# Second feed-forward product: loads pinned in program order, late operand tiles split inside the first unit, side work traced further behind its loads

## The chip, the core and the metric

The kernel runs on one core of one Trainium2 chip. TensorE (PE in the profile) multiplies matrices, with its weight loads shown apart (PEld); VectorE (DVE), ScalarE (ACT) and GpSimd (POOL) do elementwise work; SyncE (SP) issues nearly all DMAs here, one after the other. The metric is the device time of one execution in microseconds, from runs without a profiler; a further execution is profiled.

## The reference

One layer of a decoder trunk: a feed-forward block, a token mixer with two branches, a second feed-forward block, and a final norm, for 1024 prompt tokens and 64 sample tokens (8 sequences of 8). What matters here is the feed-forward block, which occurs twice:

```python
D_MODEL, D_FF = 1024, 2816

def swiglu(x, w_in, w_out):
    gu = x @ w_in
    g, u = gu[..., :D_FF], gu[..., D_FF:]
    return (jax.nn.silu(g) * u) @ w_out

x = x + 0.5 * swiglu(rmsnorm(x, norm_ffn1[l]), ffn1_w_in[l], ffn1_w_out[l])
...
x = x + mix
x = x + 0.5 * swiglu(rmsnorm(x, norm_ffn2[l]), ffn2_w_in[l], ffn2_w_out[l])
```

All values are float32. `x @ w_in` is the first product of the block, `(...) @ w_out` the second.

## The kernel before

**Number format.** A float32 operand is split into a rounded part and a remainder, both in the format that TensorE multiplies at full rate, and a product is the sum of three matmuls: rounded by rounded, remainder of x by rounded weight, rounded x by remainder of the weight. The rounded part is made by an activation on ScalarE, the remainder by a subtraction on VectorE. For weights of the second product these are `wh` and `wl` in `parts` (L782, L783); for its operand tiles they are `hh` (or `hp`) and `hr` in `split_X` (L764, L765). The activation of `split_X` is pinned, that is, queued behind everything traced before it on ScalarE.

**Tiling.** Tokens lie along the free dimension, in two halves of 512 and 576 columns; channels lie along the 128 partitions. Both products of a block are computed by a two-by-two scheme with seven products of half-size blocks instead of eight, so combinations of weights and of operands stand in place of the blocks themselves. In the second product the operand combinations have been written to DRAM (`hblock`) by the first product: eleven tiles of 128 x 544 for each of the products "1" to "7" (`NK2 = 11`, `N2 = 544`).

**The second product** (`second`) runs the products in the order 1, 2, 5, 6, 4, 7, 3. Each has four units (`m` = 0 to 3); a unit multiplies the eleven operand tiles by three chunks of weights (four, four and three tiles, `kb` = 0, 4, 8) for both halves, 66 matmuls, into two PSUM banks, and `leave` adds the result to the tiles `xt`. Product 3 is the exception: it runs its four units for one half and then for the other.

**Its weights** (`weights`, `raw`) are loaded from DRAM chunk by chunk (L771), when the unit is traced. Products 1, 2 and 4 use a block as it is. Product 5 adds two blocks on GpSimd (L800) into a tile that is held until the end; product 6 subtracts another block from the held tile (L804); `fourth` (L816), after each unit of product 4, turns the held tile into what product 3 uses; product 7 subtracts two blocks (L809). There are six buffers for raw weights and three each for `wh` and `wl`, a unit's worth.

**Its operand tiles** are loaded by `fetch_X` (L757). While unit m of a product runs, up to three tiles of the next product are fetched, at most `AHEAD[p]` in all; the rest follow at the start of that product. Its first eight tiles are split at the start of the product, the others in its first unit, before the third chunk (`kb == 8`). For product 3 all are fetched and split before its first unit.

**Old x.** The residual lies in DRAM (`xspill`). In product 6, `old` loads a quarter of it before each unit (L822), and `leave` loads another quarter into `b[:, s_]` once the unit's `add(a[:, s_], b[:, s_])` (L855) has read what stood there (L874). Product 7 loads two quarters a unit.

**The order of the work.** A scheduler reorders the instructions of each engine at compile time, by their readiness in its own model and by program order; on the chip each engine then keeps that order. This holds for SP's queue of DMAs too: an instruction there that waits for a semaphore holds up those behind it. `pin(...)` takes an instruction out of this freedom: it is queued behind the instruction traced last on the same engine. Before the change, `pin` stands at the activation of `split_X`, at the side splits and at the sums of hidden tiles and their puts.

**Side work.** A modelled clock of TensorE (`pe[0]`) advances with every matmul traced; generators wait for it (`yield 4.0` means 4 modelled us) and are stepped by `tick`. Two of them run during the first product of the first block: `turn_x` loads blocks of x (L992), waits, transposes them on TensorE (L170) and writes them to `xspill`; `part` (L312 to L321) loads weights that are used later, waits `PART_W`, splits them, writes both parts to DRAM and waits `PART_PACE`. Its 28 chunks there are followed by `finish(side)` ahead of the second product, which steps what is left without waiting.

**The last hidden pair.** The hidden tiles of the last pair of the first product (`hlast`) are put to DRAM, summed on GpSimd and put again (`hidden_odd`, `pair_sums`, L729, L708), all traced ahead of the first unit of product 1.

Of the kernel before, what the change touches and what calls it, by code (L numbers as in the profile page):

```python
# [14 lines left out]
P = 128  # L15
# [28 lines left out]
N_FP = 4  # L44
NK2, N2, HALF_AT = NFF // 2, 544, (0, 256)
H_AT, H_PACE, H_OUT, H_AGAIN, H_LOAD = 4.0, 0.5, 3.0, 100.0, 5.0
AHEAD = {'2': 11, '5': 11, '6': 8, '4': 8, '7': 10, '3': 10}
STEP = (5.0, 3.8)
STEP_S = 1.0
POST, RIPE = 1.0, 3.0  # L50
# [7 lines left out]
TURN_AT, CONST_AT = 60.0, 40.0  # L58
HP, HP_ST, HP_EV = 40, 0, 60
SETS = (((0,), (1,), (2,), (3,)), ((0, 1), (2,), (3,)))  # L60
PART_AT, PART_W, PART_PACE = 20.0, 4.0, 3.0


@with_exitstack
def tile_hybrid_pool_ssd_macaron(
# [11 lines left out]
    dma = nc.sync.dma_start  # L77
# [7 lines left out]
    def nm(s):  # L85
        uid[0] += 1
        return f"{s}_{uid[0]}"

    def act(shape=(P, 576), dt=F32, name="a"):
        return sp.tile(list(shape), dt, tag="act", bufs=N_ACT, name=nm(name))  # L90

    def pair(n, name="hl"):
        t = sp.tile([P, 2, 576], F32R, tag="pair", bufs=N_PAIR, name=nm(name))
        return t[:, 0, :n], t[:, 1, :n], t
# [16 lines left out]
    def fx(dt=F32, name="x"):  # L111
        if stage["name"] == "mix":
            return act((P, 576), dt, name)
        return stage["p"].tile([P, 592], dt, tag="fx", bufs=N_FX, name=nm(name))

    def psum(tag="ps", name="ps"):
        npd = stage["npd"]
        return stage["ps"].tile([P, 512], F32, tag=tag, bufs=npd if tag == "pd" else 8 - npd, name=nm(name))
# [35 lines left out]
    def finish(c):  # L154
        while not c.done:
            c.step()
# [8 lines left out]
    def mm(out, lhsT, rhs, start=True, stop=True, free=False):  # L165
        T.matmul(out, lhsT, rhs, start=start, stop=stop, skip_group_check=free)  # L166
        pe[0] += max(out.free_size(), 64) / 2400.0 * (1 if rhs.dtype == F32R else 4)

    def tr(out, in_, idn):
        T.transpose(out, in_, idn)  # L170
        pe[0] += 0.107
# [81 lines left out]
    xspill = [[dp.tile([P, NTOK[h]], F32, tag=f"xs{h}_{m}", name=f"xspill{h}_{m}") for m in range(KD)] for h in HALVES]  # L253
# [52 lines left out]
    pin = tc.keep_in_program_order  # L306
# [374 lines left out]
    hblock = {}  # L681
    for i in range(NK2):
        for ps_ in ("1" if i else "18", "23", "75", "46"):
            t = dp.tile([P, len(ps_), N2], F32, tag=f"hb{ps_}_{i}", name=f"hb{ps_}_{i}")
# [3 lines left out]
    even, hsums = [None, None], []  # L688
# [46 lines left out]
    hlast = []  # L735

    def second(wo, after, half):

        wv = wo.rearrange("(i two p) c -> two p i c", two=2, p=P)
# [7 lines left out]
        def fetch_X(p, n):  # L747
            for k in range(len(X[p]), min(len(X[p]) + n, NK2)):
                if k >= 4:
                    a, r = act((P, 576), F32R, "hh"), act((P, 576), name="hr")  # L750
                elif p == "1":
                    a, r = fx(F32R, "hh"), fx(name="hr")
                else:
                    a, r, _ = pair(576, "hp")
                    r = r.bitcast(F32)
                a, r = a[:, :N2], r[:, :N2]
                dma(r, hblock[p, k])  # L757
                raws.append((k, r, a))
                X[p].append((a, r.bitcast(F32R)))

        def split_X(below=NK2):
            while raws and raws[0][0] < below:
                _, r, a = raws.pop(0)
                pin(S.activation(a, r, AF.Copy))  # L764
                V.tensor_tensor(r.bitcast(F32R), r, a.bitcast(F32), op=ALU.subtract)  # L765

        def raw(par, mh, m, kb, nk, t=None):
            if t is None:
                t = sp.tile([P, 4 * P], F32, tag="wraw", bufs=N_RAW, name=nm("wraw"))[:, : nk * P]
            c0 = (mh * 4 + m) * P  # L770
            dma(t.rearrange("p (k c) -> p k c", c=P), wv[par][:, kb : kb + nk, c0 : c0 + P])  # L771
            return t

        def ring(tag, nk):
# [43 lines left out]
        def old(m, q, col):  # L818
            t = act((P, 576), name="xo")
            for h in HALVES:  # L820
                n, at = NPAIR[h], HALF_AT[h]
                dma(t[:, at : at + n], xspill[h][4 * q + m][:, col * n : (col + 1) * n])  # L822

            def put():
                for h in HALVES:
                    n, at = NPAIR[h], HALF_AT[h]
                    o = xt[h][4 * q + m][:, col * n : (col + 1) * n]
                    G.tensor_tensor(o, o, t[:, at : at + n], op=ALU.add)

            late_.append(put)  # L830

        def unit(p, m, hs, ws):
            pts = [psum("pd", "po" + p)[:, : NPAIR[h]] for h in hs]
            for kb, nk, wh, wl in ws:
                if kb and len(hs) == 2 and (p, m) == ("1", 0):
                    split_X(kb + 4)
                elif kb == 8 and len(hs) == 2:
                    split_X()
                for kk in range(nk):
                    k = kb + kk  # L840
                    for j, (W_, lo_) in enumerate(((wh, 0), (wh, 1), (wl, 0))):
                        for h, pt in zip(hs, pts):
                            at = HALF_AT[h]
                            mm(pt, W_[:, kk, :], X[p][k][lo_][:, at : at + NPAIR[h]],
                               start=k == 0 and j == 0, stop=k == NK2 - 1 and j == 2)
                    tick()
            for h, pt in zip(hs, pts):
                leave(p, m, h, pt)

        def leave(p, m, h, pt):  # L850
            n, at = NPAIR[h], HALF_AT[h]
            f, s_ = slice(0, n), slice(n, 2 * n)

            def add(out, prior):
                V.scalar_tensor_tensor(out, pt, 0.5, prior, op0=ALU.mult, op1=ALU.add)  # L855

            if p == "1":
                if T1[m] is None:
                    T1[m] = act((P, 576), name="t1")
                S.activation(T1[m][:, at : at + n], pt, AF.Copy, scale=0.5)  # L860
                return
            if p == "2":
                xt[h][m] = fx(name="x")
            elif p == "5":
                xt[h][4 + m] = fx(name="x")
            t, a, b = T1[m][:, at : at + n], xt[h][m], xt[h][4 + m]
            if p == "2":
                add(a[:, f], t)
            elif p == "5":
                add(b[:, s_], t)  # L870
            elif p == "6":
                add(a[:, s_], b[:, s_])
                add(b[:, f], t)
                dma(b[:, s_], xspill[h][4 + m][:, s_])  # L874
            elif p == "4":
                add(b[:, f], b[:, f])
                G.tensor_tensor(b[:, s_], b[:, s_], a[:, s_], op=ALU.add)
            elif p == "7":
                add(b[:, f], b[:, f])
                add(b[:, s_], b[:, s_])  # L880
            else:
                add(a[:, s_], a[:, s_])

        fetch_X("1", NK2)
        split_X(4)
        while hlast:
            hlast.pop(0)()
        while hsums:
            finish(hsums.pop(0))
        for p, nxt in zip(order[:-1], order[1:]):  # L890
            if p != "1":
                split_X(8)
            fetch_X(p, NK2)
            for m in range(4):
                if p == "6":
                    old(m, 0, 0)
                elif p == "7":
                    old(m, 1, 0)
                    old(m, 0, 1)
                unit(p, m, HALVES, weights(p, m))  # L900
                if p == "4":
                    fourth(m)
                while late_:
                    late_.pop(0)()
                n = AHEAD[nxt] - len(X[nxt])
                fetch_X(nxt, min(n, 3))
        fetch_X("3", NK2)
        split_X()
        for h in HALVES:
            half(h, xt[h])  # L910
        kept = {m: [] for m in range(4)}
# [74 lines left out]
    def turn_x(h):  # L986

        for q in range(2):
            x = [fx(name="xr") for _ in range(4)]
            for src, c0, c in blocks_of(h):  # L990
                t = fx(name="xin2")
                dma(t[:c, :512], src[:, q * 512 : (q + 1) * 512])  # L992
                yield 4.0
                pt = psum("ps", "ptr")
                for k in range(4):
                    tr(pt[:, k * P : k * P + c], t[:c, k * P : (k + 1) * P], ident[:c, :c])
                for k in range(4):
                    (V.tensor_copy if k % 2 else S.copy)(x[k][:, c0 : c0 + c], pt[:, k * P : k * P + c])
                yield 2.0
            for k in range(4):  # L1000
                dma(xspill[h][q * 4 + k], x[k][:, : NTOK[h]])
# [859 lines left out]
    for h in HALVES:  # L1861
# [4 lines left out]
        if h == 1:  # L1866
            o = []
            prep2.append((start(norm_parts(reload(0), 0, i_g2, o, 2.0)), o))
            c = prep2[0][0]
# [125 lines left out]
```

## Time and profile before

| | us |
|---|---|
| Median of 3 runs | 2934.36 |
| Lowest and highest run | 2931.92 and 2937.41 |
| The profiled execution | 2929.76 |
| Its span, first to last instruction | 2927.9 |
| Second product of the first block, first matmul | 541.1 |
| Second product of the second block, last matmul | 2911.9 |

Mean granted clock of TensorE over the span: 0.985 of full speed. DMA: 515.26 MB at a mean of 176 GB/s.

How to read it: the span is a little shorter than the time of the same execution, since the start and end of the program lie outside it. An engine's busy time says how much work it has; what a change is worth is read from the idle time of the engine that sets the end, stretch by stretch, and from who ended that idle time. In rows of the timeline the bracket at the end gives the idle time of the engine ahead of the instruction and what ended it. A name such as `PE po L166` is engine, tile written and line; L166 is the one line that issues every matmul, so the tile (`po` for the second product, `pw` for the first) tells where it belongs.

### The profile page before, as it was taken

To read this page: it belongs to the slowest core of one execution; us is meant where nothing else is said; L and a number is where in the kernel's file an instruction comes from. 1 tells how busy PE (TensorE), PEld (TensorE's weight loads), DVE (VectorE), ACT (ScalarE), POOL (GpSimd) and SP (SyncE) were. 2 spreads that over 40 slices of the span, in tenths; PEclk is the share of its full clock that TensorE was granted. 3 is DMA by queue.
4 is the path that set the end of the run, shared out by engine and by line. 5 is a ranking of instruction groups with operands and counts; after the bars stand their busy time and mean duration, and the time that the engine had idled before them with its cause. 6 is when DMAs were issued, how large, how long until landed. Compare 5 with 4: busy or idle time off the path is not lost. (4 is left out here: it accounts for less than half of the span.)

```text
span 2927.9 us, 54569 instructions
## 1 busy us (share of the span) xinstructions
PE 2787.8 (95%) x19834; PEld 2608.0 (89%) x19834; DVE 1851.4 (63%) x2848; ACT 1400.3 (48%) x3086; POOL 1367.9 (47%) x1424
## 2 busy tenths in 40 slices
PE   7999999989999999999989999898999999999998
PEld 6988999889879999999988887677999999999897
DVE  6665655667684486867666767866665444456665
ACT  5444444533454555554546566576234444444343
POOL 5456666255342364554632333323124675661651
PEclk9999999999999999999999999999999999999999
DMA  4576543778445555543366567786674332336873
GB/s 132 162 228 219 187 132 99 214 221 243 149 114 162 162 162 185 172 150 127 98 227 212 186 215 243 243 257 193 227 248 145 116 124 90 101 119 201 246 227 102
DMA packets 567438, 515.26 MB, mean 176 GB/s; under 512 B 37876, under 2 KB 436072, under 8 KB 567160
## 3 DMA queue, kind: packets, MB, share of 16 engines
q1 hardware_dynamic: 567152, 511.77, 55.8%
q8 instruction: 156, 2.56, 0.4%
q14 instruction: 114, 0.93, 0.1%
q10 hardware_dynamic: 16, 0.00, 0.0%
HBM read 363.51 MB, written 148.36 MB: 175 GB/s over the span
## 5 line engine op out<-in xcount | busy, mean ns | idle before, releaser
L166 PE MATMUL pw<-X,wh 128*128 128x288 f32 (+2 forms) x2832 | 628.3, 310 | 6.1 <-ACT v L568 3.5
L166 PEld LDWEIGHTS pw<-X,wh 128*128 128x128 f32 x2832 | 463.0, 190 | 28.7 <-ACT v L568 4.5
L166 PE MATMUL pw<-X,wl 128*128 128x288 f32 (+1 forms) x1644 | 473.6, 288 | 0.0
L452 DVE TENSOR_TENSOR wl<-s,wh 128x512 fp32r<-128x512 f32 x288 | 233.1, 810 | 258.8 <-ACT wh L451 241.7
L166 PE MATMUL pw<-hl,wh 128*128 128x256 f32 (+1 forms) x1536 | 393.0, 328 | 3.9 <-DVE t L572 3.5
L445 POOL TENSOR_TENSOR s<-wraw,wraw 128x512 f32<-128x512 f32 x144 | 201.2, 1397 | 340.5 <-DVE wl L452 218.2
L166 PE MATMUL pw<-hi,wh 128*128 128x288 f32 x1120 | 331.4, 296 | 2.6 <-DVE t L606 2.6
L166 PE MATMUL pw<-hi,wl 128*128 128x288 f32 x1120 | 330.3, 295 | 0.0
L166 PE MATMUL pw<-lo,wh 128*128 128x288 f32 x1120 | 330.0, 295 | 0.0
L166 PEld LDWEIGHTS pw<-X,wl 128*128 128x128 f32 x1644 | 312.3, 190 | 0.1
L166 PE MATMUL pw<-hl,wl 128*128 128x256 f32 x1072 | 301.0, 281 | 1.2 <-DVE wl L452 1.2
L166 PEld LDWEIGHTS pw<-hl,wh 128*128 128x128 f32 x1536 | 259.2, 189 | 25.2 <-DVE t L572 3.9
L451 ACT ACTIVATE wh<-s 128x512 fp32r<-128x512 f32 x288 | 181.2, 630 | 170.3 <-PE pw L166 147.3
L452 DVE TENSOR_TENSOR wl<-wraw,wh 128x512 fp32r<-128x512 f32 x216 | 174.0, 806 | 138.6 <-ACT wh L451 130.6
L166 PEld LDWEIGHTS pw<-hi,wh 128*128 128x128 f32 x1120 | 210.9, 188 | 9.3 <-DVE t L606 3.1
L451 ACT ACTIVATE wh<-wraw 128x512 fp32r<-128x512 f32 x216 | 135.6, 628 | 166.0 <-PE pw L166 147.4
L166 PEld LDWEIGHTS pw<-lo,wh 128*128 128x128 f32 x1120 | 211.0, 188 | 0.0
L166 PEld LDWEIGHTS pw<-hi,wl 128*128 128x128 f32 x1120 | 210.6, 188 | 0.0
L166 PEld LDWEIGHTS pw<-hl,wl 128*128 128x128 f32 x1072 | 203.4, 190 | 1.4 <-DVE wl L452 1.4
L166 PE MATMUL po<-hr,wh 128*128 128x256 f32 (+1 forms) x848 | 186.5, 290 | 6.9 <-DVE hr L765 6.7
L166 PE MATMUL po<-hh,wh 128*128 128x256 f32 (+1 forms) x848 | 185.6, 289 | 4.6 <-ACT wh L782 4.6
L166 PE MATMUL pso<-yhl,wh 128*128 128x288 f32 (+1 forms) x768 | 180.8, 338 | 5.7 <-ACT acc L1795 3.6
(400 smaller groups left out, 6832.3 us busy)
## 6 DMA issues: line engine op xcount, KB each, us to landing
wraw<-in_ffn_w_in_dram SPq DMA_DIRECT2D x188, 256.0 KB
wraw<-in_w_in_dram SPq DMA_DIRECT2D x144, 256.0 KB
wh<-part SPq DMA_DIRECT2D x116, 256.0 KB
wl<-part SPq DMA_DIRECT2D x116, 256.0 KB
hr<-hb SPq DMA_DIRECT2D x106, 272.0 KB
wraw<-in_ffn_w_out_dram SPq DMA_DIRECT2D x96, 256.0 KB
hb<-g SPq DMA_DIRECT2D x66, 288.0 KB
hb<-g SPq DMA_DIRECT2D x66, 256.0 KB
```

Of the source, the lines that this page charges most:

```text
L166: T.matmul(out, lhsT, rhs, start=start, stop=stop, skip_group_check=free)
L445: G.tensor_tensor(t, a, b, op=op)
L451: S.activation(wh, a, AF.Copy)
L452: V.tensor_tensor(wl, a, wh.bitcast(F32), op=ALU.subtract)
```

## The change

All loads of the second product are pinned in program order: raw weights (`raw`), operand tiles but those of product 1 (`fetch_X`), old x (`old`) and the reload in `leave` for product 6. The remaining splits of operand tiles are made ahead of the third weight chunk in the first unit also where a unit has one half, so product 3 splits its first eight tiles before its first unit and the others in it; `AHEAD` of product 3 goes from 10 to 8. The puts and sums of the last hidden pair move behind the first unit of product 1 (puts) and behind its third (what is left of the sums). `PART_W` goes from 4.0 to 9.0, and the wait of `turn_x` for its load from 4.0 to 8.0.

```diff
-AHEAD = {'2': 11, '5': 11, '6': 8, '4': 8, '7': 10, '3': 10}
+AHEAD = {'2': 11, '5': 11, '6': 8, '4': 8, '7': 10, '3': 8}
...
-PART_AT, PART_W, PART_PACE = 20.0, 4.0, 3.0
+PART_AT, PART_W, PART_PACE = 20.0, 9.0, 3.0
...
-                dma(r, hblock[p, k])
+                ld = dma(r, hblock[p, k])
+                if p != "1":
+                    pin(ld)
...
-            dma(t.rearrange("p (k c) -> p k c", c=P), wv[par][:, kb : kb + nk, c0 : c0 + P])
+            pin(dma(t.rearrange("p (k c) -> p k c", c=P), wv[par][:, kb : kb + nk, c0 : c0 + P]))
...
-                dma(t[:, at : at + n], xspill[h][4 * q + m][:, col * n : (col + 1) * n])
+                pin(dma(t[:, at : at + n], xspill[h][4 * q + m][:, col * n : (col + 1) * n]))
...
                 if kb and len(hs) == 2 and (p, m) == ("1", 0):
                     split_X(kb + 4)
-                elif kb == 8 and len(hs) == 2:
+                elif kb == 8:
                     split_X()
...
             elif p == "6":
                 add(a[:, s_], b[:, s_])
                 add(b[:, f], t)
-                dma(b[:, s_], xspill[h][4 + m][:, s_])
+                pin(dma(b[:, s_], xspill[h][4 + m][:, s_]))
...
         fetch_X("1", NK2)
         split_X(4)
-        while hlast:
-            hlast.pop(0)()
-        while hsums:
-            finish(hsums.pop(0))
         for p, nxt in zip(order[:-1], order[1:]):
...
                 while late_:
                     late_.pop(0)()
+                while p == "1" and hlast:
+                    hlast.pop(0)()
+                while p == "1" and m == 2 and hsums:
+                    finish(hsums.pop(0))
                 n = AHEAD[nxt] - len(X[nxt])
                 fetch_X(nxt, min(n, 3))
+        split_X(8)
         fetch_X("3", NK2)
-        split_X()
...
-                yield 4.0
+                yield 8.0
```

## The prediction

> **What bounds the kernel now.** I read the page first, then the waits of TensorE by stage, then the timeline around each long wait.
>
> ```profile
> span 2927.9 us, 54569 instructions
> ...
> PE 2787.8 (95%) x19834; PEld 2608.0 (89%) x19834; DVE 1851.4 (63%) x2848; ACT 1400.3 (48%) x3086; POOL 1367.9 (47%) x1424
> ```
>
> TensorE is busy 2787.8 of 2927.9 us, so an edit here is worth what it adds to or takes from the other 140 us, and from stretches at a reduced clock. The waits of TensorE in the stretches 500 to 900 us (second product of the first feed-forward block) and 2560 to 2928 us (of the second), and in 90 to 300 us (where x is turned), have these rows at the top (waited for: total, times, longest):
>
> ```profile
> PE po L166 <- ACT wh L782: 15.0, 4, 7.2
> ...
> PE po L166 <- ACT wh L782: 9.1, 3, 5.0
> ...
> PE ptr L170 <- DMA xin<-in_x_prompt_dram: 6.3, 3, 4.3
> ```
>
> The timeline of TensorE places the waits that the edits could reach (start, length, instruction, idle time before it):
>
> ```profile
> 613.99 0.77 PE L166 MATMUL po<-hp,wh 128*128 128x256 f32 x4 [1.34 <-ACT wh L782]
> ...
> 646.81 0.58 PE L166 MATMUL po<-hp,wh 128*128 128x256 f32 x1 [7.18 <-ACT wh L782]
> ...
> 766.83 0.58 PE L166 MATMUL po<-hh,wh 128*128 128x256 f32 x1 [4.64 <-ACT wh L782]
> ...
> 2724.11 0.39 PE L166 MATMUL po<-hp,wh 128*128 128x256 f32 x1 [1.37 <-ACT wh L782]
> ...
> 2756.30 0.58 PE L166 MATMUL po<-hp,wh 128*128 128x256 f32 x1 [5.03 <-ACT wh L782]
> ```
>
> They are the first unit of product 5 (1.34, 1.37), its last unit (7.18, 5.03) and, in the first block, the second weight chunk of product 3 (4.64). An idle stretch costs more than itself; the windows show the clock after it (columns: length, busy time by engine, granted clock, DMA share, GB/s):
>
> ```profile
> 646.81:657.04 10.23, 10.23 (x67) 10.07 (x68) 9.11 (x9) 3.61 (x7) 9.60 (x7) 0.81 0.93 292
> 657.04:665.29 8.25, 8.25 (x68) 8.25 (x68) 7.51 (x8) 3.44 (x7) 7.62 (x7) 1.00 1.08 314
> ...
> 2724.11:2732.36 8.25, 7.90 (x49) 7.68 (x49) 5.88 (x8) 2.88 (x5) 5.49 (x5) 0.79 1.06 309
> ...
> 192.00:224.00 32.00, 27.68 (x172) 25.56 (x171) 15.14 (x25) 11.23 (x26) 15.70 (x16) 0.89 0.60 198
> ```
>
> One unit (66 matmuls) takes 8.25 us at full clock and 10.23 us after the 7.18 us wait, at a mean clock of 0.81: 2.0 us per idle stretch. After only 1.37 us the clock is 0.79 too. The Trainium skill (TensorE: Matmul & The Clock Gate, "HAM oscillation — how this bites in real kernels") lets the clock fall after gaps of more than about 3.4 us; by it the wait of 1.37 would be free of the 2.0, and the sum below 2 us higher. The row decides.
>
> **What the pins remove.** Before, the scheduler may put a load that is ready ahead of an earlier one. That is what starves the last unit of product 5: the weight combinations of product 6 were made on GpSimd before it.
>
> ```profile
> L804 POOL TENSOR_TENSOR ws<-ws,wraw x12: 1016/1500/1771, 630.8 to 653.4; 128x512 f32<-128x512 f32 x8, 128x384 f32<-128x384 f32 x4
> ```
>
> All twelve combinations of product 6 start between 630.8 and 653.4, though its first unit starts only at 657.04; the three of the last unit of product 5 ran among them, and TensorE waited until 646.81. With raw, fetch_X, old and the late reload pinned in program order, product 5's loads come first. I take all of 7.18 + 5.03 + 1.34 + 1.37 = 14.9 us as gained, and three stretches of slow clock (the two in the second block, one in the first; the first unit at 613.99 I leave) at 2.0, 6 us: **-20.9**. The 4.64 us of product 3 goes too, since its tiles 8 to 10 are split behind the third weight chunk instead of ahead of the first: **-6.6** with its clock. The new place of those splits costs three activations and three subtractions within a half unit of 4.1 us: between 0 and 2, I take 0.8 a block: **+1.6**.
>
> **What the pins add.** The line that decides is L874. In product 6, unit m, it reloads old x into `b[:, s_]` after VectorE has read that half (`add(a[:, s_], b[:, s_])`, which also reads the unit's PSUM). So it cannot be issued before unit m ends on TensorE. First the waits of the SP queue (640 to 700 us), then the timelines of VectorE and SP at the end of unit 0 (665.29):
>
> ```profile
> SPq L874 <- DVE x L855: 3.1, 1, 3.1
> ...
> 665.31 0.42 DVE L855 SCALAR_TENSOR_TENSOR x<-po,x 128x256 f32<-128x256 f32 x1 [0.73 <-PE po L166]
> ...
> 665.98 0.45 DVE L855 SCALAR_TENSOR_TENSOR x<-po,x 128x288 f32<-128x288 f32 x1
> ...
> 665.76 0.34 SPq L874 DMA_DIRECT2D x<-xspill  x1
> 666.22 0.37 SPq L771 DMA_DIRECT2D ws<-in_ffn_w_out_dram  x1
> 666.69 1.42 SPq L874 DMA_DIRECT2D x<-xspill  x1
> ```
>
> Today this harms nobody: the weights of units 1 to 3 were all combined by 655 (row of L804 above). After the change everything traced behind the two reloads of unit m stands behind them in SP's queue: up to three tiles for product 4 (L757), two loads of old x (L822), then the raw weights of unit m+1 (L771). TensorE has no other ready unit. So units 1, 2 and 3 of product 6 and unit 0 of product 4 each begin with a load that could not be issued until the unit before had ended. The prices are these: SP's own time for an issue (minimum/median/maximum in ns), then steps of the chain of waits (start, length, what):
>
> ```profile
> L757 SPq DMA_DIRECT2D hr<-hb x18: 319/423/2271, 605.6 to 697.1; - x18
> ...
> L822 SPq DMA_DIRECT2D xo<-xspill x8: 319/402/1738, 649.3 to 679.8; - x8
> ...
> L771 SPq DMA_DIRECT2D wraw<-in_ffn_w_out_dram x32: 367/384/1604, 600.3 to 699.7; - x32
> ...
> 2722.13 1.28 POOL ws L800
> ...
> 2723.43 0.64 ACT wh L782
> ...
> 2724.09 1.09 DVE wl L783
> ...
> 2749.69 4.50 DMA ws<-in_ffn_w_out_dram
> ...
> 2845.95 4.86 DMA ws<-in_ffn_w_out_dram
> ```
>
> From the end of a unit: the third addition ends 1.1 us later (666.43 - 665.29), the second reload is issued by 1.6; three tiles 3 x 0.4, two loads of old x 0.8, the raw weights 0.4 bring it to 4.0; flight 4.5; the subtraction on GpSimd 1.4 (between 1.28 and the median 1.50); the cast on ScalarE 0.64; gaps between steps 0.1. TensorE starts at 10.6 us, and after four matmuls (0.5 us) waits another 0.5 for the 1.09 us of `wl`: 11.1 us for units 1 and 2, 10.7 for unit 3 (two tiles ahead of it, not three). Unit 0 of product 4 has no old x and no subtraction: 1.6 + 1.2 + 0.4 + 4.5 + 0.64 + 0.1 + 0.5 = 8.9. That is 41.8 us a block, **+83.6** in two. The clock adds 2.0 for each of eight stretches, **+16**.
>
> The flight is the weakest term. Its upper end is 4.86; below, no load can be faster than 256 KB at the 314 GB/s of the window 657.04:665.29, 0.8 us. That would take 8 x 3.7 = 30 us off. I keep 4.5, the nearest row, because the raw weights would go out behind seven other transfers. The Trainium skill (DMA: Bandwidth & Descriptors, "Latency and other measured facts") speaks of about 2 us of fixed cost per DMA; with the transfer time an estimate of 2.8 us, by which the sum would be some 14 us lower.
>
> **The other parts.** Turned x: the load is traced 8 instead of 4 modelled us ahead of its transposes. The 6.3 us of waits should go, and 2 us of the clock of 0.89 in 192 to 224: **-8** (between 0 and 6.3 + 0.11 x 32 = 9.8). That it ends later harms nothing: the first reader of the copies stands at 649.3 (row of L822). Side splits:
>
> ```profile
> L316 ACT ACTIVATE ph<-pr x28: 612/633/656, 132.3 to 383.3; 128x512 fp32r<-128x512 f32 x28
> ...
> L166 PE MATMUL po<-hh,wh x424: 278/290/583, 541.1 to 801.3; 128*128 128x256 f32 x71, 128*128 128x288 f32 x71
> ...
> 533.41 1.97 SPq L757 DMA_DIRECT2D hr<-hb x4
> ```
>
> They go at 251/27 = 9.3 us each with waits of 4 + 3; with 9 + 3 at about 15.9, so the last would come at 562, past the start of the second product at 541.1. The last two are then traced in a rush in front of it, with ScalarE's pinned casts behind fresh loads: between 0 and 2 x (4.5 + 0.64) = 10.3; I take **+4**, as both loads can be in flight at once and the first tiles of X are already on their way. The first product's raw weights now stand behind its eleven operand tiles, the last four of which go out at 533.41 to 535.38; 4.5 of flight and 0.64 of cast end at 541, where the product starts today: between 0 and 3, I take 1 a block, **+2**. The puts of the last hidden pair move behind the first unit so that the pinned loads do not stand behind them. They are covered by the 8.25 us of the unit after; were that cover gone, up to 5 us. AHEAD for product 3 takes two loads out of product 7: nothing, they are covered by its other loads.
>
> **The sum.** -20.9 - 6.6 + 1.6 + 83.6 + 16 - 8 + 4 + 2 = +71.7. The profiled execution took 2929.76 us (span 2927.9); with 71.7 it is 3001. The median of the runs, 2934.36, lies 4.6 above that execution and within 0.2%; I add nothing for it.
>
> **The rivals.**
> *Short flights (0.17).* The queue has been quiet when the raw weights go out. For: between two waits the sixteen engines idle. Against: seven transfers precede them. At the floor of 0.8 us: 3001 - 30 = 2971, and down to 2945 if the slow clock falls mostly into the idle time.
> *Drained prefetch (0.18).* The two rows below are products 6 and 4.
>
> ```profile
> 657.00:690.00 33.00, 33.00 (x267) 33.00 (x266) 31.81 (x37) 13.42 (x24) 29.16 (x24) 1.00 0.67 191
> 690.00:723.00 33.00, 33.00 (x267) 33.00 (x266) 22.15 (x34) 14.02 (x25) 10.06 (x8) 1.00 0.92 276
> ```
>
> Product 4 already runs at a DMA share of 0.92. If some 2.1 MB that go out in product 6 today are pushed into products 4 and 7, that is 2.1 MB / 276 GB/s = 7.6 us a block, with two more clock stretches each 23 us: 3024. Against: the four waits also leave the engines idle time.
> *The reload does not hold the queue (0.11), the other side.* If L874 could go out some 8 us before its unit ends, or if what follows it is not ordered behind it, units 1 to 3 start on time, and only -20.9 - 6.6 + 1.6 - 8 + 4 + 2 = -28 is left: 2902. For: the waits of SP show it held by that addition only once. Against: the addition that must come first reads the unit's own PSUM, and the second reload above went out 1.4 us after the unit's end.
> *The order hardly changes (0.03).* If the scheduler's own order had been the program's: 2930. Against: the row of L804.
>
> **How the numbers follow.** The forecast has 0.51: 3001, its own range 2980 to 3025. For 8 in 10 I reach down to 2940 (short flights and slow clock hidden) and up to 3045 (drained prefetch with a reload that goes out 1 us later, 8 us more, and 13 for units that then wait twice). Faster by over 0.2% is the third rival, 0.11; within 0.2%, about what a measurement of this kernel can tell from no change, 0.03; slower 0.86.
>
> **What would show it.** TensorE in the profile after: no wait of 5 to 7 us ahead of the last unit of product 5; four waits of 7 to 12 us in product 6 and at the start of product 4, in both blocks, on `wh L782`, with the combinations of L804 spread over the units and SP's L771 right behind L874; clock near 0.8 in each unit after them; the waits on `xin` gone; the side's last casts just before the second product. The forecast is wrong if L804's rows of units 1 to 3 still precede the end of unit 0, or if those waits are under 4 us.

## The result, and the profile after

The changed kernel takes 3019.59 us (median of 4 runs, 3014.60 to 3024.31) against 2933.14 before in the same runs (2929.97 to 2937.41): a ratio of 1.0294, 95% interval 1.0271 to 1.0316, slower. The profiled execution is one of these runs, at 3014.6 us; that of before took 2929.76, so the difference to explain is 84.8 us.

The page of the changed kernel, its first lines (span, then busy time and share of each engine):

```profile
span 3012.8 us, 54587 instructions
...
PE 2803.4 (93%) x19834; PEld 2620.9 (87%) x19834; DVE 1838.2 (61%) x2848; ACT 1398.4 (46%) x3086; POOL 1355.5 (45%) x1424
```

The instructions of TensorE are the same 19834, 15.6 us longer in sum; the other 69 us of the longer span are time in which TensorE is not busy. The waits of TensorE in 500 to 900 us, 2600 to 3012 and 90 to 300 (waited for: total, times, longest; the added lines of the change shift line numbers by two, so L784 is the cast that was L782):

```profile
PE po L166 <- ACT wh L784: 50.3, 8, 11.2
PE po L166 <- ACT hh L766: 4.1, 1, 4.1
...
PE po L166 <- ACT wh L784: 45.7, 8, 10.8
...
PE ptr L170 <- DMA xin<-in_x_prompt_dram: 2.8, 1, 2.8
```

In the timeline of TensorE the long ones stand where the forecast put them, at the start of units 1, 2 and 3 of product 6 and of unit 0 of product 4, in both blocks (the idle time ahead of each in the bracket):

```profile
659.48 1.28 PE L166 MATMUL po<-hp,wh 128*128 128x256 f32 x4 [11.17 <-ACT wh L784]
...
680.14 1.27 PE L166 MATMUL po<-hp,wh 128*128 128x256 f32 x4 [10.29 <-ACT wh L784]
...
700.08 1.28 PE L166 MATMUL po<-hp,wh 128*128 128x256 f32 x4 [9.66 <-ACT wh L784]
...
719.48 1.28 PE L166 MATMUL po<-hp,wh 128*128 128x256 f32 x4 [8.87 <-ACT wh L784]
...
790.88 0.58 PE L166 MATMUL po<-hp,wh 128*128 128x256 f32 x1 [6.82 <-ACT wh L784]
...
2815.94 1.27 PE L166 MATMUL po<-hp,wh 128*128 128x256 f32 x4 [10.79 <-ACT wh L784]
...
2837.45 1.28 PE L166 MATMUL po<-hp,wh 128*128 128x256 f32 x4 [10.79 <-ACT wh L784]
...
2857.62 1.28 PE L166 MATMUL po<-hp,wh 128*128 128x256 f32 x4 [9.92 <-ACT wh L784]
...
2876.48 0.82 PE L166 MATMUL po<-hp,wh 128*128 128x256 f32 x2 [8.48 <-ACT wh L784]
```

The four waits of products 6 and 4 in the first block are 40.0 us together, those of the second 40.0. The twelve combinations of product 6 in the first block (L804, now L806) start between 628.8 and 700.6 us, spread over the units as forecast. Of the signs that the forecast lists one did not come: the waits on `xin` are not gone, 2.8 us of 6.3 are left. The wait at 790.88 is another one, and was not foreseen: the last unit of product 7, in the first block only. Windows over the changed kernel (length, busy time of PE, PEld, DVE, ACT, POOL, granted clock, DMA share, GB/s):

```profile
790.88:799.13 8.25, 8.25 (x46) 8.25 (x47) 4.09 (x6) 4.28 (x8) 2.53 (x2) 0.66 0.78 257
...
659.48:669.68 10.20, 10.20 (x66) 10.00 (x66) 4.86 (x6) 2.80 (x5) 1.92 (x2) 0.81 0.01 2
669.68:677.92 8.24, 0.17 (x2) 0.00 (x0) 1.49 (x4) 0.00 (x0) 2.93 (x4) 0.74 0.81 245
...
729.68:771.00 41.32, 39.15 (x308) 38.46 (x307) 27.93 (x38) 15.10 (x27) 27.38 (x23) 1.00 1.02 292
```

Unit 1 of product 6 (659.48 to 669.68) takes 10.20 us at a clock of 0.81, 2.0 more than at full clock, with almost no DMA (2 GB/s). Then TensorE is idle while seven transfers and the weights go out together.

**One wait taken apart.** SP, VectorE, GpSimd and ScalarE after unit 1 of product 6, which ends at 669.68 (timelines; SP's rows are issues):

```profile
670.21 1.03 SPq L876 DMA_DIRECT2D x<-xspill  x2
671.30 0.42 SPq L757 DMA_DIRECT2D hp<-hb  x1
671.81 0.86 SPq L757 DMA_DIRECT2D hr<-hb  x2
672.76 0.86 SPq L824 DMA_DIRECT2D xo<-xspill  x2
673.71 1.48 SPq L773 DMA_DIRECT2D wraw<-in_ffn_w_out_dram  x3
...
670.43 0.45 DVE L857 SCALAR_TENSOR_TENSOR x<-po,x 128x288 f32<-128x288 f32 x1
...
678.16 3.90 POOL L806 TENSOR_TENSOR ws<-ws,wraw 128x512 f32<-128x512 f32 x3 [0.17 <-DMA wraw<-in_ffn_w_out_dram]
...
679.46 0.63 ACT L784 ACTIVATE wh<-ws 128x512 fp32r<-128x512 f32 x1 [15.86 <-POOL ws L806]
```

Read downwards it is the chain of the forecast: the third addition (670.43 to 670.88) lets the second reload out, three tiles and two loads of old x follow it, and the raw weights are issued at 673.71, 4.0 us after the unit's end. GpSimd's first subtraction starts at 678.16, after an idle time of 0.17 us that their landing ends, so the flight is between 4.3 and 4.45 us; subtraction 1.3, cast 0.63, and the next unit starts at 680.14.

**Where the 84.8 us lie.** For the table I took the start of the second product's first matmul in the first block, and the length of each product from the start of the last evacuation (the instruction that reads the result from PSUM) of the one before to the start of its own last one (us, block 1 and block 2; product 1 from the first matmul, product 3 to the last matmul of the block). The last column is the difference of both blocks together.

| | before | after | difference |
|---|---|---|---|
| start of the second product, block 1 | 541.1 | 530.1 | -11.0 |
| product 1 | 39.0, 38.8 | 41.4, 41.1 | +4.7 |
| products 2 and 5 | 77.3, 76.8 | 67.7, 67.7 | -18.7 |
| products 6 and 4 | 66.0, 66.0 | 116.2, 116.4 | +100.6 |
| products 7 and 3 | 78.2, 78.9 | 81.7, 84.6 | +9.2 |
| sum | | | +84.8 |

### The profile page after: what moved, and what is told of

It reads as the page before. It is cut to its first block, busy times and chain, and to the rows that moved or that the text cites. A ratio compares the mean times of both kernels' runs of the same rounds, so it can differ in the third digit from the quotient of the medians.

```text
span 3012.8 us, 54587 instructions
## 1 busy us (share of the span) xinstructions
PE 2803.4 (93%) x19834; PEld 2620.9 (87%) x19834; DVE 1838.2 (61%) x2848; ACT 1398.4 (46%) x3086; POOL 1355.5 (45%) x1424
## 5 line engine op out<-in xcount | busy, mean ns | idle before, releaser
L166 PE MATMUL po<-hp,wh 128*128 128x256 f32 (+1 forms) x768 | 147.4, 314 | 91.3 <-ACT wh L784 91.3
L166 PEld LDWEIGHTS po<-hp,wh 128*128 128x128 f32 x768 | 125.6, 212 | 94.0 <-ACT wh L784 94.0
```

## The experiments

Three theories on the main loss stood against each other. **Held queue:** the reload, pinned, holds SP until its unit has ended, and all that is traced behind it starts late. **Drained prefetch:** loads pushed out of product 6 fill the DMA engines later. **Something else among the edits.** Two questions on smaller terms came from the table: why products 7 and 3 lost 9 us, and what moved the first product and product 1.

**1. Pins in product 6 alone.** The kernel before, with the four loads pinned only in product 6 and unit 0 of product 4:

```diff
-dma(...)  # raw, fetch_X, old, reload in leave
+ld(...)   # pin(dma(...)) while pinned[0]
...
+pinned[0] = p == "6" or (p, m) == ("4", 0)
```

> The kernel before, with its loads pinned only while product 6 and the first unit of product 4 are traced; nothing else of the change. Theory A: the pins there suffice: eight waits of 8 to 11 us on wh at the starts of units 1 to 3 of product 6 and of unit 0 of product 4, 3010 to 3030 us. Rival B: with the pins of the other products gone the prefetch is as before at the start of product 6, and the loss is under 40 us, 2935 to 2975 us.

Measured: 3015.25 us, ratio 1.0286 (1.0268 to 1.0304): nearly the whole loss. One of its eight waits, which are 8.1 to 10.6 us long, in the timeline of TensorE:

```profile
687.83 0.58 PE L166 MATMUL po<-hp,wh 128*128 128x256 f32 x1 [10.17 <-ACT wh L786]
```

Products 6 and 4 took 114.9 and 113.2 us, close to the changed kernel's 116.2 and 116.4. Product 5, whose loads were not pinned, fell to 32.0 and 31.9 us, so pins that begin only in product 6 are enough to end the starving of its last unit: product 6's loads can no longer overtake.

**2. No pins.** The changed kernel with these four loads as they were before:

```diff
-pin(dma(...))
+dma(...)
```

> The changed kernel without its load pins in the second product: side splits, turned x, later splits, the moved puts and AHEAD of 8 stay. Theory A: all of the loss lies in the pins, and the turned x still gives its 8 to 11 us: 2918 to 2932 us, with waits of 5 to 7 us ahead of the last unit of product 5 as in the kernel before. Rival C (the moved puts and later splits cost too): 2934 to 2950 us.

Measured: 2922.39 us, ratio 0.9965 (0.9953 to 0.9977). The wait ahead of the last unit of product 5 is there again in both blocks, 7.34 and 7.52 us; the first of them:

```profile
642.96 0.58 PE L166 MATMUL po<-hp,wh 128*128 128x256 f32 x1 [7.34 <-ACT wh L782]
```

Products 7 and 3 took 70.3 and 79.7 us, 7.1 less in sum than before; this bears on the forecast's term for them, below.

**3 and 4. The reload one and two units later.** All pins stay; the reload is traced after the next unit, or the one after that, so that it stands in SP's queue behind the raw weights of that unit, and the addition that it waits for lies one or two units back:

```diff
-pin(dma(b[:, s_], xspill[h][4 + m][:, s_]))
+reloads[-1].append(lambda: pin(dma(b[:, s_], xspill[h][4 + m][:, s_])))
...
+reloads.append([])
 unit(p, m, HALVES, weights(p, m))
+if len(reloads) > 2:          # > 1: one unit later
+    for r in reloads[-3]:     # [-2]
+        r()
```

> The changed kernel (3019.6 us), with the reload of old x in product 6 traced one unit later, behind the raw weights of the next unit. Theory A (a reload that waits for the end of its unit holds SP's queue): the raw weights of unit m+1 now go out at the end of unit m-1, so of the 10.6 us from the end of a unit to the first matmul 8.25 us lie beside a unit, and each of the eight waits of 8.5 to 11.2 us falls to between 1 and 3 us; their sum falls from 80 to about 18 us, and with less slow clock the time is 2935 to 2955 us. Rival B (the pinned order as such drains the prefetch, and the transfers are the limit in products 6 and 4): the waits stay above 6 us each, and the time above 2985 us.

> The same, with the reload traced two units later. Theory A: 16.5 us of slack are more than the 10.6 us of the chain; the eight waits vanish, and with them about 80 us of waits and 18 us of slow clock: 2915 to 2930 us, so faster than the kernel before (2933.1), by the waits of product 5 and of the turned x that the change removes. Rival B: still above 2975 us, with a DMA share above 0.9 in products 6 and 4.

Measured: one unit later 2950.57 us, ratio 1.0064 (1.0045 to 1.0082); two units later 2921.59, ratio 0.9966 (0.9955 to 0.9977). With one unit the waits shrink but do not vanish (its timeline of TensorE):

```profile
661.37 0.39 PE L166 MATMUL po<-hp,wh 128*128 128x256 f32 x1 [2.27 <-ACT wh L785]
...
693.92 0.58 PE L166 MATMUL po<-hp,wh 128*128 128x256 f32 x1 [3.23 <-ACT wh L785]
```

With two units products 6 and 4 take 68.2 and 67.6 us. The same loads in the same pinned order, with only the reload moved, cost 98 us less: the held queue, not the traffic, is the loss. With the reload out of the way the pins on all loads bring nothing in the total, 2921.59 us against 2922.39 without any: what they gain in product 5 they lose elsewhere, as the next runs show.

**5. No pins from product 7 on.** With the reload two units later, products 7 and 3 still took 82.5 and 84.9 us. SP's timeline of that kernel showed why in the first block:

```profile
727.01 0.48 SPq L774 DMA_DIRECT2D wraw<-in_ffn_w_out_dram  x1
727.54 9.40 SPq L1045 DMA_DIRECT2D xspill<-x  x4
737.04 0.88 SPq L758 DMA_DIRECT2D hr<-hb  x2
737.97 3.05 SPq L825 DMA_DIRECT2D xo<-xspill  x4
741.12 0.38 SPq L774 DMA_DIRECT2D ws<-in_ffn_w_out_dram  x1
```

Four stores of finished x (`squares`, not pinned), which wait for additions on VectorE (4.4 us) and GpSimd (3.2 us), hold the queue for 9.4 us, and the raw weights of the last unit of product 7 stand behind them, behind two tiles and four loads of old x. TensorE then waited:

```profile
748.38 0.58 PE L166 MATMUL po<-hp,wh 128*128 128x256 f32 x1 [7.38 <-ACT wh L785]
```

```diff
+on[0] = p in "12564"          # loads pinned only while on[0]
...
+on[0] = False                 # ahead of product 3
```

> Reload traced two units later as in defer2 (2921.6 us), and no load of product 7 and later is pinned. In defer2 a wait of 7.4 us stands ahead of the last unit of product 7 in the first block, and in the second one transposes and casts wait 1.1 to 2.2 us each on sums of old x. Theory A2 (pinned loads of product 7 stand behind unpinned work that the scheduler could move ahead of them): these waits go, products 7 and 3 take 70 instead of 82.5 us in the first block and 79.5 instead of 85 in the second, 2900 to 2910 us. Rival B2 (product 7 is at the limit of the DMA engines in any order): products 7 and 3 change by less than 4 us, 2916 to 2924 us.

Measured: 2907.61 us, ratio 0.9900 (0.9881 to 0.9918). Products 7 and 3: 72.2 and 78.6 us. In its SP timeline (the loads go through a helper here, so they all have its line, L750) the raw weights come first, then tiles and old x, then the stores:

```profile
728.84 0.48 SPq L750 DMA_DIRECT2D wraw<-in_ffn_w_out_dram  x1
729.41 0.91 SPq L750 DMA_DIRECT2D hr<-hb  x2
730.37 1.85 SPq L750 DMA_DIRECT2D xo<-xspill  x4
732.26 1.45 SPq L1049 DMA_DIRECT2D xspill<-x  x3
```

**6. The stores pinned too.** The reload two units later, all pins, and the store in `squares` as `pin(dma(...))`, so that it cannot move ahead of loads traced earlier.

> defer2 with one more pin: the stores of x to DRAM that follow the second product of the first block stay in program order too, so they cannot stand ahead of product 7's loads in SP's queue. Theory A2: the wait of 7.4 us ahead of the last unit of product 7 falls under 2 us in the first block, nothing changes in the second: 2911 to 2917 us. Rival B2: the wait stays above 5 us, 2918 to 2924 us.

Measured: 2919.48 us, ratio 0.9944 (0.9927 to 0.9961), between the two theories: the wait fell only by half, and products 7 and 3 took 78.4 and 85.1 us, against 82.5 and 84.9.

```profile
742.84 0.77 PE L166 MATMUL po<-hp,wh 128*128 128x256 f32 x4 [3.83 <-ACT wh L785]
```

The stores were therefore one part of it, 4.1 of the 10.3 us that run 5 gained in the first block. That tiles and old x still stand ahead of the raw weights in pinned order would fit the rest, but no run separated that.

**7. Product 3's splits.** The best kernel (number 12) with product 3 as before: ten tiles fetched ahead, and all eleven split before its first unit.

```diff
-AHEAD = {... '3': 8}
+AHEAD = {... '3': 10}
...
-                elif kb == 8:
+                elif kb == 8 and len(hs) == 2:
...
-        split_X(8)
         fetch_X("3", NK2)
+        split_X()
```

> The best kernel so far (reload two units later, pins in products 5, 6 and 4 alone, gap of 7; 2896.4 us in its own runs), with product 3 put back as it was before the change: ten of its operand tiles fetched in product 7, not eight, and all eleven split ahead of its first weight chunk. Question: is the wait of 4.64 us at the second weight chunk of product 3 ended by the moved splits, as the prediction had it (-6.6 us in one block, +1.6 in both)? Theory, yes: the wait is back in one block, products 7 and 3 together are 4 to 7 us longer in it than the 72.1 us of the best kernel, and the time is 2899 to 2903. Rival: products 7 and 3 got shorter because the load of that chunk no longer stands behind stores, whatever the splits; then they stay within 1.5 us and so does the time.

Measured: 2893.30 us, ratio 0.9868 (0.9851 to 0.9886), beside 0.9870 (0.9842 to 0.9899) of the kernel it was made from. Products 7 and 3 took 72.2 and 77.9 us against 72.2 and 78.5, and no wait like the 4.64 us of before came back. The rival's number is right: in this kernel the place of the splits moves nothing measurable. The trace of the kernel before tells what the 4.64 us were. A store of finished x that waited for GpSimd held SP's queue; the loads of product 3's last two tiles went out behind it; and ScalarE's cast of the second weight chunk stood behind the pinned splits of these tiles (a row of SP's waits from 755 to 763 us, then rows of the timelines of SP and ScalarE):

```profile
SPq L1038 <- POOL x L828: 4.4, 1, 4.4
...
760.95 0.92 SPq L757 DMA_DIRECT2D hr<-hb  x2
...
763.99 0.66 ACT L764 ACTIVATE hh<-hr 128x544 fp32r<-128x544 f32 x1 [6.33 <-DMA hr<-hb]
```

In run 7 these two loads are issued at 722.44 and ScalarE waits only 0.86 us for them, so the splits in their old place hold nothing up. In run 2, with the splits in their new place and all loads free, the wait is gone too. Whether the new place alone would end it in the kernel before, no run tried.

**8 and 9. The side's two waits, each alone in the kernel before.** Once only `yield 4.0` to `yield 8.0` in `turn_x`, once only `PART_W` 4.0 to 9.0.

> The kernel before with the wait of the turned x at 8 instead of 4 and nothing else. The prediction's term: waits on xin fall from 6.3 to under 3.5 us, and the second product of the first block starts 8 to 11 us earlier; 2922 to 2926 us against 2932.5. If the transposes stand later for another reason, or the gain came from the side splits: 2929 to 2934 us.

> The kernel before with the wait of the side splits at 9 instead of 4 and nothing else. The prediction's term: the last splits are made in a rush ahead of the second product; waits of 4 to 6 us on the first split operand tiles appear in the first block, 2934 to 2939 us. Rival: the waits of TensorE in the first product (2.3 on ScalarE and 3.5 on VectorE at 228 and 261 us), which are behind casts that wait for their load, go with it and outweigh the rush: 2926 to 2932 us.

Measured: the longer wait of `turn_x` 2927.78 us, ratio 0.9973 (0.9961 to 0.9985), in neither of its two ranges; `PART_W` 2930.96, ratio 0.9985 (0.9973 to 0.9996), in the rival's range. The waits on `xin` did not fall with the first (6.8 us against 6.3; its timeline has this one):

```profile
213.43 0.47 PE L170 MATMUL ptr<-ident,xin 128*128 128x128 f32 x1 [5.62 <-DMA xin<-in_x_prompt_dram]
```

From its first matmul on `pw` to the start of the second product the first product took 438.8 us before, 436.0 with the first edit, 433.9 with the second, 428.7 with all. So `PART_W`, which had been forecast as a cost alone, gives more of this gain than the wait of `turn_x`. The rush came with it, as forecast: waits of 5.33 us on `hh` and 3.57 us on `hr` at the start of the second product, which leave less of the 4.9 us in the total.

**10 to 12. Product 1 and the rush.** The reload two units later, pins only in products 5, 6 and 4; the same with the puts of the last hidden pair ahead of the first unit again; the first again with `PART_W` at 7.0, by which the side's 28 chunks end before the first product does.

```diff
+on[0] = p in "564"            # 10, 11 and 12
...
-PART_AT, PART_W, PART_PACE = 20.0, 9.0, 3.0
+PART_AT, PART_W, PART_PACE = 20.0, 7.0, 3.0    # 12
```

> The reload is traced two units later, and only the loads of products 5, 6 and 4 stand in pinned order; those of products 1, 7 and 3 don't. The twin with pins in products 1, 5, 6 and 4 took 2907.6 us. Question: what makes product 1 some 2.3 us a block longer after the change (41.4 against 39.0). Theory, pinned loads: ScalarE's casts of the units' weights stand behind the evacuation of the unit before, 1.16 us three times; without pins product 1 is back at 39 us and the time is 2901 to 2905. Rival, the puts of the last hidden pair that now lie behind the first unit: product 1 stays at 41 to 42 in both blocks, and the time stays at 2905 to 2910.

> As the run before it, and the puts of the last hidden pair stand ahead of the first unit again, as before the change. By the theory (pinned loads) nothing moves, within 2 us of the run before. By the rival (the moved puts) product 1 falls from 41 to 42 us to 39 and the time by 3 to 5 us. If the puts delay the start of the second product, as they may where loads are pinned, the first evacuation of it comes later by up to 5 us.

> As the first of these three, with a gap of 7 instead of 9 modelled us between a side chunk's load and its split, so that the last chunks aren't traced in a rush ahead of the second product. Theory: the waits of 4.08 and 2.06 us at the start of the second product of the first block go, and with them 4 to 6 us less the slow clock they leave: the time is 2 to 6 us under the first run. Rival: the rush only moves work that the first product would carry anyway, as the run with the wider gap alone showed (its first product got 4.9 us shorter): within 1.5 us of the first run.

Measured: 2902.23 us, ratio 0.9894 (0.9860 to 0.9927); 2904.45, ratio 0.9901 (0.9873 to 0.9928); 2896.36, ratio 0.9870 (0.9842 to 0.9899). ScalarE's timeline at the end of unit 1 of product 1, first in the changed kernel, then in run 10:

```profile
551.38 0.68 ACT L862 ACTIVATE t<-po 128x256 f32<-128x256 f32 x2 [5.64 <-PE po L166]
551.95 1.56 ACT L784 ACTIVATE wh<-wraw 128x512 fp32r<-128x512 f32 x3
```

```profile
552.54 0.63 ACT L787 ACTIVATE wh<-wraw 128x512 fp32r<-128x512 f32 x1 [2.37 <-PE po L166]
554.79 0.53 ACT L787 ACTIVATE wh<-wraw 128x384 fp32r<-128x384 f32 x1 [1.62 <-PE po L166]
555.22 0.67 ACT L865 ACTIVATE t<-po 128x256 f32<-128x256 f32 x2
```

With pinned loads the cast of the next unit's first weights stands behind the evacuation `t<-po` of the unit before, and TensorE waits 1.16 us at the start of units 2 and 3 of product 1 and of unit 0 of product 2; without pins the casts come first and the three waits are gone in both blocks. From run 5 to run 10, products 1 and 2 fell from 41.4 + 34.7 to 38.9 + 32.8 us in block 1 and from 42.1 + 34.7 to 40.1 + 32.8 in block 2, about 8 us in all. Little of that is left in the total: the medians differ by 5.4 us, the ratios to before, 0.9900 and 0.9894, overlap, and the two profiled executions took the same (2901.90 and 2902.64 us). One reason is that the second product started 2.9 us later, behind a longer rush (6.37 us ahead of its first matmul, not 4.08). The puts' old place gained nothing (product 1 took 41.8 and 40.5 us with it), so behind the first unit they cost nothing, at least where product 1's loads are free. The side's casts, in the changed kernel and in run 12 (duration minimum/median/maximum in ns, first and last start):

```profile
L316 ACT ACTIVATE ph<-pr x28: 614/632/637, 133.7 to 524.9; 128x512 fp32r<-128x512 f32 x28
```

```profile
L316 ACT ACTIVATE ph<-pr x14: 615/632/636, 308.9 to 482.1; 128x512 fp32r<-128x512 f32 x14
```

With a wait of 7 the last one (the second row counts those from 300 us on) comes at 482.1 and no longer in front of the second product, which starts at 524.6 instead of 533.0: 8.4 us, of which 5.9 are left in the total. Runs 12 and 7 beat both kernels of this study, by 1.3% against before and some 4% against after (2896.36 / 3019.59 = 0.959).

## Why the prediction was right, and where it was not

Forecast 3001 us from a sum of +71.7 on the profiled execution; measured +84.8 there, and 3019.59 as median, inside the likeliest case's own range. The forecast's terms sorted into the stages of the table: the turned x and the rush lie before the second product's first matmul, the raw weights of product 1 in product 1.

| stage | forecast | measured |
|---|---|---|
| turned x -8, rush +4 | -4 | -11.0 |
| product 1, raw weights | +2 | +4.7 |
| products 2 and 5 | -20.9 | -18.7 |
| products 6 and 4: 83.6 + 16 | +99.6 | +100.6 |
| products 7 and 3: -6.6 + 1.6 | -5.0 | +9.2 |
| sum | +71.7 | +84.8 |

**The held reload, +83.6 and +16: right, in mechanism, place and size.** Runs 1, 3 and 4 show it by putting the cost nearly alone into the kernel before and by taking it alone out of the one after. The eight waits make 80.0 us. Of the 83.6, 4.0 were for a second wait of 0.5 us on `wl` in each unit, which did not come: at the slow clock the first four matmuls last 1.28 us, longer than the 1.08 us of `wl`. That leaves 79.6 against 80.0. Eight slow units at 2.0 make 16; the last 5 us of the 100.6 are small pieces, such as a wait of 0.85 us on `wl` in unit 0 of product 6 in each block. The weakest term, a flight of 4.5 us, came out at 4.3 to 4.45. The estimate by the Trainium skill (DMA: Bandwidth & Descriptors, "Latency and other measured facts") was 2.8; this load, behind seven others, took some 1.5 us longer than that.

**Rivals.** Short flights held half its premise, a quiet queue (2 GB/s in the window from 659.48), but seven transfers went out just ahead of the weights and the flight was not short; how long a load by itself would take there, no run shows. (The floor of 0.8 us took the 314 GB/s of one window for a limit; the window from 2813.22 in the last section has 339, which moves the floor by less than 0.1 us.) That the reload does not hold the queue is excluded by the row of L876 and by run 4. Drained prefetch named a total close to the measured one, 3024, but not for its reason: the DMA share in product 7 did rise, to 1.02 in the window from 729.68, yet TensorE was busy 39.15 of 41.32 us there, and run 4, with the same loads, lost nothing in product 4.

**Product 5, -20.9: right.** The four waits and the slow clock behind them are gone, and after the change product 5 has no wait on TensorE in either block. The 2.2 by which products 2 and 5 gained less fit a cost that the sum did not have, the wait of 1.16 us at the start of product 2 in each block. The cause is narrower than "product 5's loads come first" through all four pins: run 1 got 17.2 of the 18.7 us from pins that begin in product 6.

**Products 7 and 3, -6.6 + 1.6: the step that failed is a term that the sum put at nothing, the pinned loads of product 7.** With the moved splits but without load pins (run 2) the two products took 7.1 us less than before, near the forecast's 5.0. With the pins they took 81.7 + 84.6 us, 16.3 more than without. Run 5 finds nearly the same price by taking the pins out from product 7 on: 16.6 (82.5 + 84.9 - 72.2 - 78.6). In the first block it is 10.3 us, with the wait of 7.4 us in it; run 6 gives 4.1 of them to the unpinned stores, queue entries that the forecast had not looked for, and the rest is open. The 6.3 us of the second block are not assigned to one wait. The -6.6 itself has the right mechanism, pinned splits ahead of the cast, but left out why these were late (a store that held the tiles' loads), and run 7 shows that the wait can also end with the splits where they were. The 14.2 us by which this row of the table is off are more than the 13.1 by which the sum fell short of the profiled execution; the other rows nearly cancel.

**Turned x, -8: about the right size for the wrong reason, which is luck.** The longer wait alone brought 2.8 us of the first product and left the `xin` waits; `PART_W` alone brought 4.9. Why a longer wait between a chunk's load and its split helps the first product was not tried by itself. **The rush, +4:** it exists, and begins with the wait of 4.1 us on `hh L766`; in run 10, where that wait is 6.37 us, its removal (run 12) starts the second product 8.4 us earlier. **Product 1, +2:** 4.7 were measured, and the wait was not the one named. No wait on its first raw weights shows in the profile; it was ScalarE's casts behind the evacuation, 1.16 us twice a block in product 1.

**Moved puts, 0: right** by run 11, where product 1's loads are free; with pinned loads it was not tried.

## What to carry to other kernels

An order fixed by hand is only as good as its slowest entry: before pinning a queue, look through it for an entry that waits on the result of the work in progress, and count everything traced behind it as starting after that work. If the entry is not needed soon, move it behind the next units' loads; here that one edit turned 2.9% slower into 0.3% faster. But compare with no pins at all, which was 0.3% faster too: pins paid only where loads had overtaken. Without them in products 7 and 3 the kernel came to 1.0% faster than before, and with a shorter wait of the side splits to 1.3%. Entries outside the fixed order, such as the stores here, count as well, since they may be placed in front of it.

## What the runs showed of the hardware

The clock of TensorE fell after much shorter idle time than the long waits, and not by length alone. In each of the fourteen traces the records of the granted clock change only on a grid of 3.41 us. The windows below are cut on that grid (columns as above). The first five are from the kernel with the reload one unit later, around waits of 1.51 us ahead of 2805.50 and of 2.03 us ahead of 2817.80:

```profile
2802.98:2806.40 3.42, 1.91 (x14) 1.51 (x13) 1.34 (x3) 1.40 (x3) 0.00 (x0) 1.00 0.70 204
2806.40:2809.81 3.41, 3.41 (x16) 3.41 (x17) 3.41 (x8) 1.98 (x4) 1.08 (x1) 0.50 0.27 73
...
2813.22:2816.64 3.42, 2.55 (x21) 2.33 (x19) 0.79 (x2) 0.00 (x0) 2.27 (x2) 1.00 1.09 339
2816.64:2820.05 3.41, 2.25 (x16) 2.07 (x17) 2.06 (x4) 2.61 (x5) 0.41 (x1) 1.00 1.17 297
2820.05:2823.46 3.41, 3.41 (x30) 3.41 (x29) 3.41 (x3) 0.82 (x2) 3.41 (x3) 1.00 1.11 340
```

The wait of 1.51 us lies in one window, TensorE is busy for 1.91 of its 3.41 us, and the next window has half the clock. The wait of 2.03 us is divided by a boundary, which leaves 2.55 and 2.25 us busy, and the clock stays full. In run 10 two waits of 1.22 and 0.84 us, ahead of 723.33 and 724.94, fall into one window:

```profile
722.18:725.59 3.41, 1.42 (x9) 1.20 (x10) 3.41 (x6) 0.63 (x1) 2.41 (x3) 1.00 0.37 108
725.59:729.00 3.41, 3.41 (x17) 3.41 (x17) 0.85 (x3) 1.31 (x3) 3.41 (x4) 0.50 0.63 177
```

I counted such windows over the second products of all fourteen traces, those at full clock. Where TensorE was idle for 1.9 us or more in the window, the next one was slow in all 49 cases; where it was idle for less than 1.5 us, in none of 1943; between, in 6 of 14. So what counts here is the idle time within one window, and the same wait can be free or not by where it falls. It fits the forecast's rows: the wait of 1.37 us at 2724.11 drew a slow clock, and the one of 1.34 us at 613.99 did not (idle time in its window 1.2 us, against 1.7). What decides between 1.5 and 1.9 us stays open. The slow stretches were mostly 3.4, 6.8 or 10.2 us long, and mostly 10.2 after waits over 6 us. The Trainium skill (TensorE: Matmul & The Clock Gate, "HAM oscillation — how this bites in real kernels") names gaps of more than about 3.4 us; here the slow clock came well below that.
